# Second product of the last layer's Strassen down projection: P2 ahead of P3, and the P5 weight sums twelve units later

## The chip, the cores and the metric

One core of one Trainium2 chip runs the whole program. The metric is the device time of one execution in microseconds (us). The kernel before was run three times (median 2460.65 us), and one further execution was profiled.

## The reference

A bidirectional encoder trunk of two layers (`DEPTH = 2`) on 1040 rows (16 meta tokens and 1024 of the sequence), width 1024. Each layer is a hybrid mixer (a chunked gated delta rule beside a gated short convolution), then a SwiGLU feed-forward block with `D_FF = 2816` columns, that is 22 tiles of 128. Only the feed-forward block matters here:

```python
def swiglu(h, w_gate_up, w_down):
    gate, up = jnp.split(h @ w_gate_up.astype(h.dtype), 2, axis=-1)
    return (jax.nn.silu(gate) * up) @ w_down.astype(h.dtype)
...
    for l in range(DEPTH):
        h = h + hybrid_mixer(rmsnorm(h, norm1_w[l]), w_in[l], ...)
        h = h + swiglu(rmsnorm(h, norm2_w[l]), w_gate_up[l], w_down[l])
    h = rmsnorm(h, final_norm_w)
    return h[:, N_META:]
```

## The kernel before

**Arithmetic.** Every fp32 product is made of three fp32r matmuls: both operands are split into a rounded part (`hi`) and the remainder (`lo`), and `hi*hi + hi*lo + lo*hi` goes into one PSUM bank. The split of a tile is one ScalarE copy (`hi`) and one VectorE subtraction (`lo`). In the down projection these are lines L1320 and L1321 for weights (128x384, three tiles of 128) and L1368 and L1369 for activations (128x512); the three matmuls are L1688, L1690 and L1691.

**The down projection.** 18 of its 22 row tiles go through a two-level product scheme of Strassen's kind in Winograd's form: the 8 output tiles are two halves of four, the 18 inner tiles are two halves of nine (`NP = 9`), and the 1024 columns of the last layer are two halves of 512 (`NB = 512`, one PSUM bank, `NJ = 1`). Seven products `P1` to `P7` replace eight. The other four row tiles are multiplied plainly afterwards, together with the final norm.

**Units.** A product is 12 units: three blocks `b` of three inner tiles, and in each block four output tiles `m`. A unit is nine matmuls of 512 columns. `UNITS` lists all 84 in the order of `SEVEN`, which before is P5, P3, P2, P1, P6, P7, P4 in both layers. P5, P2 and P1 start new PSUM banks at `b == 0`, four for the four `m`. P3 goes on adding in the banks of P5 after P5 has been read out, and P6, P7 and P4 in those of P1. The read-outs are VectorE additions into the residual rows (L1695), four for each product, in the units of its last block. `pbank()` goes round the eight banks, so P5 and P1 get the same four and P2 gets the other four.

**Operands.** These are the preparations on VectorE that matter here, beside the splits:

- `s_sum("S2", n)`, L1279: loads a third weight block (192 KB, into a ring `s_room` of eight places) and subtracts it from the weight sum `S` which P5 has used. Twelve of them, one for each `n`. P3 and later P6 use the result.
- `w_unit` of a P3 unit, L1317: subtracts that sum `S` from a freshly loaded weight block. Twelve. The weights of P2 are plain loaded blocks (`a_raw`) without a subtraction; both come from the same ring of buffers.
- `t_pair` of a P3 tile, L1371: after the split, makes the second activation sum, which P6 uses, in place. Nine, one for each inner tile. P2 and P3 load their nine activation tiles through the same ring of seven places (`b_room`), from the rows that the gate/up part wrote to DRAM (`ad`).

**Order.** Work is written out unit by unit: `under[u]` lists what is issued ahead of the matmuls of unit `u`. Weights are split `LEAD = 5` units ahead of use. The twelve S2 sums stand under units 3 to 14; P3's first weights are made under unit 7. The helper `behind` puts such VectorE work of unit `u` after the read-out of unit `u - 2`, where there is one. A planner then lays out the queue of each engine from that order, as priorities, and its own estimates of durations, and the program holds the queues as laid out. Ahead of the first units stands the end of the gate/up part, whose last rows are finished by L1442 to L1445 and whose last banks are read out by L1573 to L1586.

```python
            if p in ("P5", "P6", "P7"):
                r = s_raw(n)
            elif p == "P3":
                r = a_raw(0, 1, n)
                behind(tt(out=r, in0=r, in1=s_raw(n), op=ALU.subtract))
            else:
                r = a_raw(*{"P2": (0, 1), "P1": (0, 0), "P4": (1, 1)}[p], n)
```

The part of the second layer runs from about 2209 us to 2398.8 us of the span. Its first units are interleaved with the last matmuls of gate/up until about 2230 us.

Of the kernel before, what the change touches and what calls it, by code (L numbers as in the profile page):

```python
# [42 lines left out]
def trunk(ctx: ExitStack, tc: tile.TileContext, xT, w_in, w_ba, w_out, w_gu, w_dn,  # L43
# [8 lines left out]
    def nm(p):  # L52
        cnt[0] += 1
        return f"{p}_{cnt[0]}"
# [13 lines left out]
    def bank(tag):  # L68
        return psp.tile([128, 512], F32, tag=tag, bufs={"acc": 3, "a": 1, "f": 2, "b": 2}[tag], name=nm("p" + tag))
# [15 lines left out]
    def after(ins, prev):  # L85

        if prev is not None:
            tc.add_manual_dep(ins.ins, prev.ins.name, dep, reason="order")
        return ins
# [51 lines left out]
    def wload(src, nk):  # L141

        res = []
        step = min(nk, WK)
        for k0 in range(0, nk, step):
            kk = min(step, nk - k0)
            hi = wp.tile([128, WK, 128], F32R, tag="whi", name=nm("whi"))
            lo = wp.tile([128, WK, 128], F32R, tag="wlo", name=nm("wlo"))
            wsplit(src[:, k0:k0 + kk, :], hi[:, 0:kk, :], lo[:, 0:kk, :])
            for k in range(kk):  # L150
                res.append((hi[:, k, :], lo[:, k, :]))
        return res
# [161 lines left out]
    for l in range(DEPTH):  # L314
        last = l == DEPTH - 1
# [722 lines left out]
        def half(ap, z):  # L1038

            v = ap.rearrange("p (g e) -> p g e", g=4) if len(ap.shape) == 2 else ap.rearrange("p k (g e) -> p k g e", g=4)  # L1040
            s = slice(1, 3) if z == 0 else slice(0, 4, 3)
            return v[:, s, :] if len(ap.shape) == 2 else v[:, :, s, :]
# [67 lines left out]
        def pbank():  # L1110
            bn[0] += 1
            return bank(("acc", "f", "acc", "b", "acc", "f", "b", "a")[bn[0] % 8])
# [21 lines left out]
        def part(t, z, j):  # L1134

            v = half(t[:, o0:L], z)
            return v[:, j, :] if NJ == 2 else v
# [6 lines left out]
        def pin(ps):  # L1144
            return loc(ps, 0)
# [86 lines left out]

        SEVEN = ("P5", "P3", "P2", "P1", "P6", "P7", "P4")
        BH = {"P2": (1, 0), "P3": (1, 1), "P1": (0, 0), "P7": (0, 0), "P4": (1, 0)}
        NBK = NP // 3
        UNITS = [(p, b, m) for p in SEVEN for b in range(NBK) for m in range(4)]
        td = dram.tile([NP, 128, NB], F32, name=nm("td"))
# [3 lines left out]
        def behind(ins):  # L1243

            return after(ins, read_out.get(at[0] - 2))
# [6 lines left out]
        def a_load(to, dh, fh, n):  # L1252
            f0 = NF + NP * fh + 3 * (n // 4)
            dma(to.rearrange("p (k e) -> p k e", k=3), w_dn[l, 4 * dh + n % 4, :, f0:f0 + 3, :])
            return to

        def a_raw(dh, fh, n):
            nr[0] += 1
            return a_load(raw4("raw" if nr[0] % 7 in (0, 3) else "ck2").rearrange("p a b -> p (a b)")[:, 0:384], dh, fh, n)

        def s_raw(n):
            r = n // 2
            if ("S", r) not in dw:
                dw["S", r] = row(Y[1], F32, 3) if r < 3 else c4k("S") if r < 5 else row(X[1] + "f")
            return dw["S", r][:, 384 * (n % 2):384 * (n % 2) + 384]

        def s_room():

            nr[2] += 1
            r = nr[2] // 2 % 4  # L1270
            if ("X", r) not in dw:
                dw["X", r] = row(X[1], F32, 3) if r < 3 else row(Y[1] + "f")
            return dw["X", r][:, 384 * (nr[2] % 2):384 * (nr[2] % 2) + 384]

        def s_sum(which, n):

            S = s_raw(n)
            if which == "S2":
                behind(tt(out=S, in0=S, in1=a_load(s_room(), 0, 0, n), op=ALU.subtract))  # L1279
            else:  # L1280
                behind(tt(out=S, in0=a_raw(1, 1, n), in1=S, op=ALU.subtract))
# [61 lines left out]
        def t_slot(t):  # L1343

            o = 2 * NB * (t % 4)
            return [dw["T", t // 4 % 2][:, o + NB * q:o + NB * q + NB] for q in range(2)]

        def t_load(t):
            p, i = SEVEN[t // NP], t % NP
            if p in BH:  # L1350
                dw["b", t] = b_load(*BH[p], i)
                held[t] = NB * ((nr[1] - 1) % 7)
            elif p == "P5":
                dma(t_raw(i), td[i])

        def t_pair(t):
            p, i = SEVEN[t // NP], t % NP
            hi, lo = t_slot(t)
            r = dw.pop(("b", t), None)
            held.pop(t, None)  # L1360
            if p in ("P5", "P6"):
                r = t_raw(i)
            elif p == "P7":
                behind(tt(out=r, in0=t_raw(i), in1=r, op=ALU.subtract))
            elif p == "P4":
                b21, r = r, t_raw(i)
                behind(tt(out=r, in0=b21, in1=r, op=ALU.subtract))
            act(out=hi, in_=r, func=AF.Copy)  # L1368
            behind(tt(out=lo, in0=r, in1=hi.bitcast(F32), op=ALU.subtract))  # L1369
            if p == "P3":  # L1370
                tt(out=t_raw(i), in0=r, in1=t_raw(i), op=ALU.subtract)  # L1371
# [2 lines left out]
        LEAD = 5  # L1374
        under = [[] for _ in UNITS]
        for n in range(12):
            under[n + 3].append(lambda n=n: s_sum("S2", n))
            under[n + 49].append(lambda n=n: s_sum("S3", n))
        for t in range(4, NP * 7):
            u = max(0, 4 * (t // 3 - 1) - 1 + t % 3)  # L1380
# [75 lines left out]
        for f in range(FT):  # L1456
# [45 lines left out]
            ps = {}  # L1502
# [142 lines left out]
        def last_weights(m):  # L1645
            if not fin_w:
                fin_w.append(flat(Y[0][2], F32R)[:, 0:4096].rearrange("p (m k e) -> p m k e", m=8, k=4))
                rows = [row(Y[1], F32R, 3) for _ in range(3)] + [row(Y[1] + "f", F32R)]
                fin_w.append([r[:, 512 * q:512 * q + 512].rearrange("p (k e) -> p k e", k=4) for r in rows for q in range(2)])
            hi, lo = fin_w[0][:, m], fin_w[1][m]  # L1650
            wsplit(w_dn[l, m, :, 0:NF, :], hi, lo, raw4(("raw", "ck2")[m % 2]))
            wds.append([(hi[:, k], lo[:, k]) for k in range(4)])
# [6 lines left out]
        bks, begun = {}, {}  # L1659
# [4 lines left out]
        for u, (p, b, m) in enumerate(UNITS):  # L1664
            if b == 1 and p in FIRST:
                dh, z = FIRST[p]
                q = 4 * dh + m
                after(dma(half(hr[q][:, o0:L], z), half(hd[q][:, o0:L], z)), begun[u - 2])
            at[0] = u
            for fn in under[u]:  # L1670
                fn()
            if last and u == 77:
                for q in range(KT):
                    last_weights(q)
            if not last and u >= len(UNITS) - 2:
                pre["dn", u - len(UNITS) + 2] = wload(w_dn[l, u - len(UNITS) + 2, :, 0:NF, :], NF)
            if p in ("P5", "P2", "P1") and b == 0:
                for j in range(NJ):
                    bks[m, j] = pbank()
            wh, wl = dw.pop(("w", u))  # L1680
            for j in range(NJ):
                ps = bks[m, j]
                cs = slice(CW * j, CW * j + CW)
                for k in range(3):
                    th, tl = t_slot(3 * (u // 4) + k)
                    st = p in ("P2", "P5", "P1") and b == 0 and k == 0
                    en = b == NBK - 1 and k == 2
                    one = mm(ps[:, :CW], wh[:, k, :], th[:, cs], start=st, stop=False, skip_group_check=True)  # L1688
                    begun.setdefault(u, one)
                    mm(ps[:, :CW], wh[:, k, :], tl[:, cs], start=False, stop=False, skip_group_check=True)  # L1690
                    mm(ps[:, :CW], wl[:, k, :], th[:, cs], start=False, stop=en, skip_group_check=True)  # L1691
                if b == NBK - 1:
                    dh, z, op = TO[p]
                    h = part(hr[4 * dh + m], z, j)
                    read_out[u] = tt(out=h, in0=pin(ps), in1=h, op=op)  # L1695
# [9 lines left out]
        else:  # L1705
# [22 lines left out]
            for (n0, n1) in FIN:  # L1728
                e = (n1 - n0) // 4
                sv = ss[:, n0:n1]  # L1730
                ps = bank("a")
# [100 lines left out]
```

## Time and profile before

| | |
|---|---|
| three runs | 2459.36, 2460.65, 2460.89 us |
| the profiled execution | 2459.55 us |
| its span, first to last instruction | 2457.7 us |
| TensorE busy (matmul) | 2435.8 us, 99% of the span |
| VectorE busy | 1827.4 us, 74% |
| ScalarE busy | 1079.5 us, 44% |
| mean DMA rate | 137 GB/s |

The 1.85 us between the span and the execution's time lie around the first and the last instruction. In the rows that follow, PE is TensorE, PEld its weight loads, DVE VectorE, ACT ScalarE, SP the queue that issues the DMAs. A timeline row gives start and duration in us, engine, line, operation, what is written from what, and in brackets the idle time of the engine before it and what ended that. A stretch row gives the stretch and its length, then for each engine the busy time and the instructions in it, the granted TensorE clock, the mean busy share of the DMA engines and GB/s. Durations of neighbouring instructions overlap; what one costs its engine is the distance from start to start.

### The profile page before, as it was taken

How to read it: one execution, taken by the hardware profiler on the slowest of the kernel's cores; microseconds unless marked ns; L12 is line 12 of the kernel's file. 1: busy time of each engine (PE TensorE's matmuls, PEld its weight loads, DVE VectorE, ACT ScalarE, POOL GpSimd, SP SyncE). 2: the span in 40 equal slices, each digit the busy share in tenths (PEclk: the TensorE clock that was granted, in tenths of full speed). 3: DMA queues.
4: the chain of work that ended last, by engine and by line, in shares of the span. 5: the costliest groups of instructions: out<-in, count | busy, mean ns of one | idle time of the engine just before them, and what ended most of it. 6: DMA issues, size and time to landing. Idle time of an engine off the chain costs nothing. (4 is left out here: it accounts for less than half of the span.)

```text
span 2457.7 us, 45163 instructions
## 1 busy us (share of the span) xinstructions
PE 2435.8 (99%) x17590; PEld 2254.1 (92%) x17590; DVE 1827.4 (74%) x3416; ACT 1079.5 (44%) x2020; POOL 65.8 (3%) x157
## 2 busy tenths in 40 slices
PE   9999999999999999999999999999999999999998
PEld 8999999999999999999999988999988888887887
DVE  6888345768888877877657984457798888878775
ACT  6654433536333333344445543345463333334544
POOL 0130000000000000000000200000000000000002
PEclk9999999999999999999999999999999999999999
DMA  4445344534323224675224453546343222347641
GB/s 134 155 154 178 122 140 151 165 111 147 102 91 105 93 77 137 216 237 154 89 83 148 160 170 107 157 133 205 112 142 108 91 95 99 123 136 245 198 134 69
DMA packets 201898, 336.32 MB, mean 137 GB/s; under 512 B 23468, under 2 KB 88420, under 8 KB 201684
## 3 DMA queue, kind: packets, MB, share of 16 engines
q1 hardware_dynamic: 173572, 294.88, 37.3%
q10 hardware_dynamic: 25936, 34.19, 4.4%
q0 software_dynamic: 2176, 4.36, 0.6%
q8 instruction: 138, 2.26, 0.4%
q14 instruction: 76, 0.62, 0.1%
HBM read 251.36 MB, written 81.99 MB: 136 GB/s over the span
## 5 line engine op out<-in xcount | busy, mean ns | idle before, releaser
L168 PE MATMUL pacc<-a,whi 128*128 128x346 f32 (+1 forms) x800 | 260.6, 327 | 0.9 <-ACT a L188 0.9
L170 PE MATMUL pacc<-a,wlo 128*128 128x346 f32 (+1 forms) x800 | 259.3, 325 | 0.0
L168 PE MATMUL pacc<-b,whi 128*128 128x346 f32 (+2 forms) x672 | 232.7, 347 | 0.0
L170 PE MATMUL pacc<-b,wlo 128*128 128x346 f32 (+2 forms) x672 | 231.6, 346 | 0.2 <-DVE wlo L139 0.2
L169 PE MATMUL pacc<-a,whi 128*128 128x346 f32 (+1 forms) x681 | 221.9, 326 | 0.2 <-DVE a L189 0.2
L138 ACT ACTIVATE whi<-raw 128x512 fp32r<-128x512 f32 x166 | 104.4, 631 | 238.4 <-PE pacc L169 193.5
L169 PE MATMUL pacc<-b,whi 128*128 128x346 f32 (+2 forms) x580 | 200.2, 346 | 0.0
L139 DVE TENSOR_TENSOR wlo<-raw,whi 128x512 fp32r<-128x512 f32 x166 | 114.0, 688 | 55.9 <-ACT whi L138 55.1
L168 PEld LDWEIGHTS pacc<-a,whi 128*128 128x128 f32 x800 | 150.8, 189 | 3.2 <-ACT a L188 1.2
L170 PEld LDWEIGHTS pacc<-a,wlo 128*128 128x128 f32 x800 | 150.9, 189 | 1.2 <-issue 0.8
L170 PEld LDWEIGHTS pacc<-b,wlo 128*128 128x128 f32 x672 | 126.5, 188 | 10.3 <-issue 1.7
L168 PEld LDWEIGHTS pacc<-b,whi 128*128 128x128 f32 x672 | 126.6, 188 | 10.1 <-issue 1.0
L169 PEld LDWEIGHTS pacc<-a,whi 128*128 128x128 f32 x681 | 128.5, 189 | 3.8 <-issue 2.1
L169 PEld LDWEIGHTS pacc<-b,whi 128*128 128x128 f32 x580 | 109.2, 188 | 7.8 <-issue 1.0
L1104 ACT ACTIVATE whi<-rw 128x512 fp32r<-128x512 f32 (+1 forms) x84 | 51.5, 621 | 104.1 <-PE pacc L1125 24.5
L1104 ACT ACTIVATE b<-rw 128x512 fp32r<-128x512 f32 (+1 forms) x63 | 38.8, 621 | 85.1 <-PE pb L1125 28.3
L1104 ACT ACTIVATE a<-rw 128x512 fp32r<-128x512 f32 (+1 forms) x63 | 38.8, 621 | 79.3 <-PE pacc L1125 22.5
L331 DVE TENSOR_TENSOR b<-pacc,rstd 128x346 f32<-128x346 f32 (+1 forms) x63 | 32.3, 512 | 48.5 <-PE pacc L170 45.9
L331 DVE TENSOR_TENSOR a<-pacc,rstd 128x346 f32<-128x346 f32 (+2 forms) x59 | 32.6, 553 | 41.5 <-PE pacc L170 41.4
L1105 DVE TENSOR_TENSOR wlo<-rw,whi 128x512 fp32r<-128x512 f32 (+1 forms) x84 | 56.1, 672 | 5.4 <-ACT whi L1104 5.1
L1688 PE MATMUL pacc<-P,whi 128*128 128x260 f32 (+1 forms) x177 | 59.6, 337 | 0.3 <-ACT whi L1320 0.3
L1691 PE MATMUL pacc<-P,wlo 128*128 128x260 f32 (+1 forms) x177 | 59.5, 336 | 0.0
(1143 smaller groups left out, 7948.6 us busy)
## 6 DMA issues: line engine op xcount, KB each, us to landing
raw<-in_w_in SPq DMA_DIRECT2D x110, 256.0 KB, 3.1
raw<-in_w_gu SPq DMA_DIRECT2D x108, 256.0 KB, 3.1
rw<-in_w_gu SPq DMA_DIRECT2D x88, 256.0 KB, 2.7
rw<-in_w_dn SPq DMA_DIRECT2D x90, 192.0 KB, 2.5
rec<-vkd SPq DMA_DIRECT2D x61, 256.0 KB, 4.3
raw<-in_w_out SPq DMA_DIRECT2D x48, 256.0 KB, 2.9
b<-ad SPq DMA_DIRECT2D x45, 260.0 KB, 4.4
a<-ad SPq DMA_DIRECT2D x45, 256.0 KB, 4.0
```

What stands on the lines that cost most here:

```text
L138: whi_done[0] = hasten(wpr, lambda: act(out=hi, in_=raw[:, 0:kk, :], func=AF.Copy))
L139: whi_done[1] = hasten(wpr, lambda: tt(out=lo, in0=raw[:, 0:kk, :], in1=hi.bitcast(F32), op=ALU.subtract))
L168: mm(ps[:, :n], wh, xh[:, n0:n1], start=(i == 0), stop=False)
L169: mm(ps[:, :n], wh, xl[:, n0:n1], start=False, stop=False)
L170: last_mm[0] = mm(ps[:, :n], wl, xh[:, n0:n1], start=False, stop=(i == K - 1))
L331: tt(out=t[:, n0:n1], in0=ps, in1=rstd[:, n0:n1], op=ALU.mult)
L1104: hasten(wpr, lambda: act(out=hi, in_=src, func=AF.Copy))
L1105: hasten(wpr, lambda: tt(out=lo, in0=src, in1=hi.bitcast(F32), op=ALU.subtract))
L1688: one = mm(ps[:, :CW], wh[:, k, :], th[:, cs], start=st, stop=False, skip_group_check=True)
L1691: mm(ps[:, :CW], wl[:, k, :], th[:, cs], start=False, stop=en, skip_group_check=True)
```

## The change

In the last layer alone, the order of the seven products becomes P5, P2, P3, P1, P6, P7, P4: the third comes second. The twelve S2 sums are listed under units 15 to 26 instead of 3 to 14. The banks of a product are looked up by whether it is P2, since P2 now runs while P5's banks wait for P3. The first layer keeps its order.

```diff
-        SEVEN = ("P5", "P3", "P2", "P1", "P6", "P7", "P4")
+        SEVEN = ("P5", "P2", "P3", "P1", "P6", "P7", "P4") if last else ("P5", "P3", "P2", "P1", "P6", "P7", "P4")
...
-            under[n + 3].append(lambda n=n: s_sum("S2", n))
+            under[n + (15 if last else 3)].append(lambda n=n: s_sum("S2", n))
...
-                    bks[m, j] = pbank()
+                    bks[p == "P2", m, j] = pbank()
...
-                ps = bks[m, j]
+                ps = bks[p == "P2", m, j]
```

## The prediction

> **What bounds the kernel now.** I read the page first, then the table of stretches over the last layer's down projection, cut at the starts of its products, and then the timelines of the stretch that stands out.
>
> ```profile
> span 2457.7 us, 45163 instructions
> PE 2435.8 (99%) x17590; PEld 2254.1 (92%) x17590; DVE 1827.4 (74%) x3416; ACT 1079.5 (44%) x2020; POOL 65.8 (3%) x157
> ```
>
> ```profile
> core 0: us, PE busy (x) PEld busy (x) DVE busy (x) ACT busy (x) POOL busy (x), PEclk, DMA share, GB/s
> 2209.00:2230.60 21.60, 21.60 (x95) 17.59 (x94) 18.76 (x30) 6.27 (x12) 0.00 (x0) 1.00 0.56 185
> 2230.60:2247.30 16.70, 16.70 (x74) 13.56 (x73) 15.02 (x28) 7.66 (x14) 0.00 (x0) 1.00 0.99 332
> 2247.30:2274.30 27.00, 25.85 (x110) 20.09 (x109) 24.40 (x46) 12.97 (x26) 0.00 (x0) 1.00 0.82 254
> 2274.30:2299.10 24.80, 24.80 (x109) 20.26 (x108) 15.33 (x26) 11.25 (x22) 0.00 (x0) 1.00 0.70 223
> 2299.10:2324.10 25.00, 25.00 (x110) 20.32 (x110) 19.97 (x34) 13.94 (x25) 0.00 (x0) 1.00 0.64 203
> ...
> 2374.00:2398.80 24.80, 24.80 (x109) 20.21 (x108) 15.71 (x27) 9.69 (x18) 1.33 (x5) 1.00 0.33 95
> ```
>
> TensorE bounds the program, so a change here is worth only what it takes off, or adds to, TensorE's idle time. The rows are: the seam with gate/up, the rest of P5, P3, P2, P1 and, after those left out, P4. P3's stretch is the only one with idle TensorE time (25.85 of 27.00 us), and there VectorE is busy 24.40 us; in P2's it is busy 15.33 of 24.80 us. The stretches of P1 and P4 have no idle TensorE time.
>
> Inside P3's stretch the timelines of TensorE, ScalarE and VectorE read:
>
> ```profile
> 2253.82 0.40 PE L1690 MATMUL pb<-P,a 128*128 128x512 f32 x1
> 2254.91 0.50 PE L1688 MATMUL pf<-P,a 128*128 128x512 f32 x1 [0.69 <-ACT a L1320]
> 2255.25 0.39 PE L1690 MATMUL pf<-P,a 128*128 128x512 f32 x1
> 2255.98 0.50 PE L1688 MATMUL pacc<-P,whi 128*128 128x512 f32 x1 [0.34 <-ACT whi L1320]
> 2256.32 0.40 PE L1690 MATMUL pacc<-P,whi 128*128 128x512 f32 x1
> 2256.83 0.51 PE L1691 MATMUL pb<-P,a 128*128 128x512 f32 x1
> 2257.18 0.40 PE L1688 MATMUL pb<-P,a 128*128 128x512 f32 x1
> ...
> 2258.35 0.40 PE L1691 MATMUL pb<-P,a 128*128 128x512 f32 x1
> ```
>
> ```profile
> 2254.33 0.52 ACT L1320 ACTIVATE a<-rw 128x384 fp32r<-128x384 f32 x1 [2.08 <-DVE rw L1317]
> 2255.40 0.94 ACT L1320 ACTIVATE whi<-rw 128x384 fp32r<-128x384 f32 x2 [0.55 <-DVE rw L1317]
> ```
>
> ```profile
> 2253.28 0.55 DVE L1321 TENSOR_TENSOR a<-rw,a 128x384 fp32r<-128x384 f32 x1
> 2253.75 0.55 DVE L1317 TENSOR_TENSOR rw<-rw,a 128x384 f32<-128x384 f32 x1
> 2254.22 0.68 DVE L1369 TENSOR_TENSOR P<-a,P 128x512 fp32r<-128x512 f32 x1
> 2254.82 0.55 DVE L1317 TENSOR_TENSOR rw<-rw,a 128x384 f32<-128x384 f32 x1
> ```
>
> TensorE waits for a split weight (L1320), the split waits for P3's weight subtraction (L1317), and that one stands in a VectorE queue without a gap: VectorE is late, by its amount of work. This is the one stall that the change can take away.
>
> **What the stall is worth.** From 2257.18 to 2258.35 five steps take 1.17 us, 0.234 us each. From 2253.82 to 2257.18 six steps take 3.36 us; at 0.234 they would take 1.40. The stall costs 1.96 us. This is more than the idle time shown (0.69 + 0.34), since the first matmul after each gap also takes longer and its successor starts later. Nothing else in this part can be gained: the other quoted stretches have no idle TensorE time. By the Trainium skill (TensorE: Matmul & The Clock Gate, "Wait — 56ns, not 53.3ns?") warm matmuls of 512 columns follow each other every 215.7 ns; with that figure the stall would be 2.07 us, an estimate, but the rows here say 0.234 us and they decide.
>
> **What moves away from the stall.** Stretches of VectorE for the three kinds of sums, one row pair each for L1279 (S2 sums), L1317 (P3's weights) and L1371 (the activation sums made with P3); the first row of a pair ends where the stall begins:
>
> ```profile
> 2209.00:2254.90 45.90, 5.34 (x10) 1.00 0.73 237
> 2254.90:2274.30 19.40, 1.10 (x2) 1.00 0.89 283
> 2209.00:2254.90 45.90, 3.92 (x8) 1.00 0.73 237
> 2254.90:2274.30 19.40, 2.68 (x5) 1.00 0.89 283
> 2209.00:2254.90 45.90, 6.17 (x9) 1.00 0.73 237
> 2254.90:2274.30 19.40, 0.00 (x0) 1.00 0.89 283
> ```
>
> An instruction of 384 columns occupies VectorE for 0.47 us (2253.28 to 2253.75) and one of 512 for 0.60 us (2254.22 to 2254.82). There are 12, 12 and 9 of them in all; one of L1317 crosses the cut and is in both its rows. By the stall VectorE had worked on 10 + 8 of the former and 9 of the latter: 18 x 0.47 + 9 x 0.60 = 13.9 us of work that P5 and P2 do not need. With P2 second, all of it belongs to a product that starts 24.8 us later. What P2 itself needs by then, one weight split a unit and three activation splits in four units, P3 needs as well, so it adds nothing. VectorE was late by about 2 us and is relieved of 13.9. I take the stall as gone, −1.96 us; the bounds are 0 (the relief is undone by something unseen) and −1.96.
>
> **What then falls due later.** P3's stage now has all 24 sums of 0.47 and nine of 0.60, 16.7 us, on top of what a plain product needs, 15.33 us (P2's row): 32.0 us of work in 24.8 us of TensorE time, 7.2 us too much. But P2's stage ahead of it leaves 24.80 − 15.33 = 9.5 us of VectorE free, and the two together need 47.4 of 49.6 us. The S2 sums can use that room: they stand under units 15 to 26, their ring has eight places, and each needs only its load and a sum that P5 has finished with. P3's weights are due five units ahead of use. The length of a unit follows from the starts of P2 and P1:
>
> ```profile
> 2274.27 0.39 PE L1688 MATMUL pb<-P,whi 128*128 128x512 f32 x1
> 2299.15 0.39 PE L1688 MATMUL pacc<-P,whi 128*128 128x512 f32 x1
> ```
>
> That is 24.88 us for 12 units, 2.07 us each, so the lead is 10.4 us, more than the 7.2 us even if no sum ran ahead. In the stage of before VectorE came from two stretches without slack (18.76 of 21.60 and 15.02 of 16.70 us) and still lost only 1.96 us. I cost this at 0, between 0 and +7.2 us; the cover is the lead, and if that were gone entirely the price would be the full 7.2.
>
> **Loads.** Each S2 sum brings a DMA of 192 KB, twelve in all, 2.36 MB, about 7.1 us at the 332 GB/s of the stretch from 2230.60, where the DMA engines are 0.99 busy. They leave that stretch for P2's stage, which at 0.70 of 24.8 us has 7.4 us free: just enough, and it need not all fit, since the ring lets loads go early. What waits for such a load is the sum itself, and behind it in VectorE's order the splits for P2 and P2's read-outs. On SP's queue the S2 loads pass P2's activation and weight loads, which now stand ahead of them. I cost this at 0 (a late load: up to the lead again).
>
> **Banks.** P2 now opens its banks twelve units earlier, at about 2247 us. They were gate/up's, and the last one is read out here:
>
> ```profile
> 2230.42 0.60 ACT L1582 ACTIVATE a3f<-pa 128x512 f32<-128x512 f32 x1
> ```
>
> That is 16 us earlier, so it costs nothing. P1 opens the banks that P3 has just left: before, P2's 12 units lay between, now there are three units (6.2 us) from the end of P3's unit for one `m` to P1's first matmul on the same bank. How late a read-out can be is seen at the worst one before, P5's last:
>
> ```profile
> 2247.08 0.40 PE L1691 MATMUL pf<-P,a 128*128 128x512 f32 x1
> ```
>
> ```profile
> 2251.61 0.68 DVE L1695 TENSOR_TENSOR b<-pf,b 128x512 f32<-128x512 f32 x1
> ```
>
> It ended 4.8 us after its last matmul, with VectorE full. This fits in 6.2 us, so the new wait costs 0; with VectorE as late as 7.2 us it would cost 1.0 us. In return P5's read-outs lose their haste, since P3 comes 12 units later. The reloads of residual rows ahead of each product's read-out change places with their product and cost nothing either way.
>
> **The sum.** −1.96 + 0 + 0 + 0 = −1.96 us. On the profiled execution that is 2459.55 − 1.96 = 2457.6 us, span 2455.7 us. That execution lies 1.1 us under the median of the three runs, so for a median I take 2460.65 − 1.96 = 2458.7 us. TensorE has no idle time between the stall and the end of the last quoted stretch, so nothing catches up with the gain before 2398.8 us; the plain end after it depends on TensorE's arrival in the same way. A measurement of this kernel can tell about 0.2% (4.9 us) from no change, and the gain is below that.
>
> **The rivals.** First, the stall moves instead of going: P3's stage, 12 units later, has the same weight sums and more, and the planner may leave them as late as before. For it speaks that 32.0 us of work still stand against 24.8; against it, the 9.5 us free just ahead. Its price is the old stall again, so the net is 0: 2460.65 us. I give it 0.18.
>
> Second, slower: VectorE enters P3's stage with nothing done ahead, because a sum waiting for its load holds the queue through P2's stage. Then 7.2 us of excess work meets a lead that is used up, and the result is 2460.65 − 1.96 + 7.2 = 2465.9 us. It is slower than now from the point where less than 7.2 − 1.96 = 5.2 us of the excess is covered away, and by more than 4.9 us only if nearly the whole lead is lost. For it speaks the tight sum of DMA time (7.1 of 7.4 us); against it, that the loads ran at 332 GB/s where they had to. With other disorder of a newly laid out queue I give it 0.11. By the Trainium skill (TensorE: Matmul & The Clock Gate, "HAM oscillation — how this bites in real kernels") TensorE gaps over about 3.4 us also lose the clock; a single gap of 7.2 us would then cost more than here. The stall above is shorter and its stretch keeps a clock of 1.00, so no row here tests that.
>
> Third, a gain above 4.9 us. The stretches of this part hold no more than the 1.96 us; it would have to come from the layout of the queues in the plain end, and no row speaks for it: 0.04. That the change does not do what it says (the planner runs the sums early anyway, in holes) leaves the forecast standing, since P2 does not wait for them.
>
> **How the numbers follow.** The forecast has 0.67: 2458.7 us, with its own range from 2457.2 to 2460.9, the spread of the runs and a stall only partly gone. With the first rival it makes 0.85 within 0.2%; slower 0.11, faster 0.04. For 8 in 10 the range takes in the first rival and part of the way to the second: 2456.8 to 2463.0.
>
> **What would show it.** In the profile after, the TensorE timeline from 2247 us on should have steps of 0.234 us without a gap, P2's matmuls following P5's, and no L1317 before about 2255 us. In P2's stage VectorE should be fuller than 15.33 us by S2 sums, and P3's stage, from about 2272 us, should have idle TensorE time of 0 with L1317 ahead of its splits. P1's first matmuls should not wait for L1695. The forecast is wrong if a TensorE gap released by L1320 or L1321 stands in P3's stage, by the length of that gap, or if one stands where the rows of before show none.

## The result: 0.14% faster, TensorE's stall gone, and more saved than the stall of one profile

In 22 runs of each kernel in turn, the median went from 2459.02 us (2456.30 to 2461.77) to 2454.82 us (2453.10 to 2462.09), 4.2 us less. The ratio is 0.9986, with a 95% interval from 0.9980 to 0.9991: between 2.2 and 4.9 us faster. The change thus stays within the 0.2% that the prediction called no change, but the time lies 2.0 us under its range (2456.8 to 2463.0).

The first profiled execution of the changed kernel was the slowest of all its runs (2462.09 us; half clock for 3.41 us at 56 and at 210 us, where the queues of both kernels are still the same). A second profile of it, of 2454.03 us, is read here. Its stretches from 2226.90 us are the rest of P5, then P2, P3 and P1, which answer to the table of before:

```profile
core 0: us, PE busy (x) PEld busy (x) DVE busy (x) ACT busy (x) POOL busy (x), PEclk, DMA share, GB/s
2226.90:2243.90 17.00, 17.00 (x75) 13.83 (x74) 12.79 (x23) 8.62 (x17) 0.00 (x0) 1.00 0.85 281
2243.90:2268.80 24.90, 24.90 (x109) 20.27 (x108) 22.93 (x43) 10.02 (x20) 0.00 (x0) 1.00 0.75 233
2268.80:2293.70 24.90, 24.90 (x109) 20.27 (x108) 18.71 (x35) 12.12 (x24) 0.00 (x0) 1.00 0.74 232
2293.70:2318.30 24.60, 24.60 (x108) 20.01 (x107) 19.68 (x34) 13.19 (x25) 0.00 (x0) 1.00 0.64 201
```

TensorE has no idle time in any of them; before, P3's stretch had 25.85 us busy of 27.00. VectorE's work is levelled: P3's stage holds 18.71 us instead of 24.40, P2's 22.93 instead of 15.33, and the DMA engines are 0.85 busy in the stretch of P5 where they were at 0.99. The seam from P3 to P1 on the timelines of TensorE and VectorE, in the same profile:

```profile
2293.49 0.40 PE L1691 MATMUL pf<-P,a 128*128 128x512 f32 x1
2293.73 0.39 PE L1688 MATMUL pacc<-P,whi 128*128 128x512 f32 x1
```

```profile
2289.99 0.68 DVE L1695 TENSOR_TENSOR b<-pacc,b 128x512 f32<-128x512 f32 x1
...
2294.84 0.68 DVE L1695 TENSOR_TENSOR b<-pf,b 128x512 f32<-128x512 f32 x1
```

P1 starts 0.24 us after P3's last matmul, on a bank that was read out 3 us earlier. P3's last read-out ends 1.6 us after its matmul, where P5's had taken 4.8 us before.

From its first to its last matmul (L1688 to L1691) the part takes 187.58 us in all three profiles of the changed kernel. In the profile of before that the prediction used it took 189.61 us: 2.03 us saved, by the sum's 1.96. The measured median moved twice as far, 4.2 us. The experiments below look for the rest.

### The profile page after: what moved, and what is told of

Same layout as the page of the kernel before. It is cut to its first block, busy times and chain, and to the rows that moved or that the text cites. A ratio compares the mean times of both kernels' runs of the same rounds, so it can differ in the third digit from the quotient of the medians.

```text
span 2460.3 us, 45153 instructions
## 1 busy us (share of the span) xinstructions
PE 2438.8 (99%) x17590; PEld 2257.0 (92%) x17590; DVE 1826.4 (74%) x3416; ACT 1078.8 (44%) x2020; POOL 66.3 (3%) x157
## 5 line engine op out<-in xcount | busy, mean ns | idle before, releaser
L331 DVE TENSOR_TENSOR a<-pacc,rstd 128x346 f32<-128x346 f32 (+2 forms) x59 | 32.6, 553 | 41.7 <-PE pacc L170 41.6
L1691 PE MATMUL pacc<-P,wlo 128*128 128x260 f32 (+1 forms) x177 | 59.5, 336 | 0.0
L1688 PE MATMUL pacc<-P,whi 128*128 128x260 f32 (+1 forms) x177 | 59.4, 336 | 0.0
```

What stands on the lines that cost most here:

```text
L331: tt(out=t[:, n0:n1], in0=ps, in1=rstd[:, n0:n1], op=ALU.mult)
```

## The experiments

Each one is compared with the kernel before in the same session. "Part" is the time from the first to the last matmul of the scheme in the second layer, read from the one profile of each.

| kernel | part, us | ratio to before | 95% interval |
|---|---|---|---|
| before, again | 189.92 | 0.9996 | 0.9988 to 1.0005 |
| changed, again | 187.58 | 0.9981 | 0.9973 to 0.9990 |
| changed, third time | 187.58 | 0.9990 | 0.9981 to 0.9998 |
| order only | 187.55 | 0.9984 | 0.9975 to 0.9992 |
| before without S2 loads | 187.78 | 0.9988 | 0.9980 to 0.9996 |
| before without second activation sums | 187.56 | 0.9988 | 0.9979 to 0.9996 |
| before with 24 more VectorE instructions | 200.77 | 1.0039 | 1.0026 to 1.0051 |
| changed with the same 24 | 191.40 | 1.0005 | 0.9996 to 1.0014 |

**Both kernels again.** No edit.

> The kernel before, unchanged, once more, for the spread of its stall at the head of P3. Work theory (VectorE is late by its amount of work, and by how much differs between executions): ratio 1.000, and a TensorE stall in P3's stretch that differs clearly from the 1.96 us of the first profile, 3 to 5 us where the execution is slower. Rival (the stall is always 2 us and the rest of the 0.14% comes from elsewhere): ratio 1.000 and again 2 us of stall.

> The changed kernel, unchanged, once more, for a profile with the clock granted as in the kernel before. Work theory: ratio 0.998 to 0.999, no TensorE gap from the start of P5's own stretch to the end of P4, the part about 187.6 us long from its first to its last matmul as in the first profile. Rival: the part is as long, and a further 1.5 to 2 us are saved after it, in the plain end, or before it.

Before again had the same stall, 2.3 us (part 189.92). The changed kernel again had none. After the part, from its last matmul to the end of the span, the two profiles take 59.20 and 59.10 us, so nothing is saved in the plain end. This left the further difference unexplained by either theory as put.

**The order without the later sums.**

```diff
-            under[n + (15 if last else 3)].append(lambda n=n: s_sum("S2", n))
+            under[n + 3].append(lambda n=n: s_sum("S2", n))
```

> P2 second as in the change, but the twelve S2 sums listed under units 3 to 14 as before. Work theory: 8 weight subtractions and 9 activation sums still leave the stage before P2, 3.8 + 5.4 = 9.2 us of VectorE time, against a lateness of 2 to 5 us: the stall is gone and the ratio is that of the change, 0.9980 to 0.9991. Load theory (the twelve loads of 192 KB in the stretch with the DMA engines 0.99 busy make the weights late): part of the stall stays, ratio 0.999 to 1.000.

The stall is gone, as with the whole change, at a ratio that cannot be told from it. The order alone does it. The listing of the sums matters little, because the planner does not hold to it: in the changed kernel eight of the twelve sums (L1279) start between 2226.34 and 2243.48 us, ahead of P2's stage, which is as many as their ring has places; two more start at the end of P2's stage and two in P3's.

**The kernel before without the loads of the S2 sums.**

```diff
-                behind(tt(out=S, in0=S, in1=a_load(s_room(), 0, 0, n), op=ALU.subtract))
+                behind(tt(out=S, in0=S, in1=s_raw(n - 1 if n else 1) if last else a_load(s_room(), 0, 0, n), op=ALU.subtract))
```

> The kernel before, but each S2 sum of the last layer takes a weight sum that lies in SBUF already in place of its loaded block (the twelve loads of 192 KB are left out; VectorE's work is the same). Work theory: the stall stays, ratio 0.9995 to 1.0005. Load theory: the stall goes or is halved, ratio 0.998 to 0.9992.

The stall is 0.2 us, against the work theory: VectorE's work is the same and the stall has gone nevertheless. VectorE's timeline shows what became of the sums:

```profile
2211.13 0.55 DVE L1279 TENSOR_TENSOR a<-a 128x384 f32<-128x384 f32 x1
...
2212.67 0.55 DVE L1279 TENSOR_TENSOR a<-a 128x384 f32<-128x384 f32 x1
2213.14 0.55 DVE L1317 TENSOR_TENSOR rw<-rw,a 128x384 f32<-128x384 f32 x1
2213.61 0.55 DVE L1279 TENSOR_TENSOR a<-a,a 128x384 f32<-128x384 f32 x1
2214.07 0.55 DVE L1317 TENSOR_TENSOR rw<-rw,a 128x384 f32<-128x384 f32 x1
```

They stand in the seam with gate/up, from 2211 us on, and P3's weight subtractions follow them at once. In the kernel before, the same timeline reads:

```profile
2215.87 0.69 DVE L1371 TENSOR_TENSOR a<-a,a 128x512 f32<-128x512 f32 x1 [2.75 <-DMA a<-ad]
...
2234.53 0.55 DVE L1279 TENSOR_TENSOR a<-a,b 128x384 f32<-128x384 f32 x1
...
2236.60 0.55 DVE L1317 TENSOR_TENSOR rw<-rw,a 128x384 f32<-128x384 f32 x1
...
2239.30 0.69 DVE L1371 TENSOR_TENSOR a<-a,a 128x512 f32<-128x512 f32 x1 [1.68 <-DMA a<-ad]
```

The first S2 sum starts at 2234.53 us and the first weight subtraction at 2236.60. VectorE stood idle for 2.75 us ahead of 2215.87 and for 1.68 us ahead of 2239.30. At the first of these there was no sum to fill it with, since the loads for the sums were issued only from 2229.95 us on. So the loads have a part in the stall, by when they come. It was not DMA time that held the first of them back. Shortly ahead of their issue the DMA engines were 0.20 busy:

```profile
2224.20:2227.70 3.50, 3.50 (x17) 2.83 (x16) 3.50 (x6) 0.51 (x1) 0.00 (x0) 1.00 0.20 56
```

In that stretch SP's queue waited 3.5 us for VectorE to finish a row of gate/up (L1445) that it had to store (L1449). Whether the buffers of the loads were free any sooner, and whether DMA time made the later loads late, was not told apart.

**The kernel before without the second activation sums.**

```diff
-            if p == "P3":
+            if p == "P3" and not last:
                 tt(out=t_raw(i), in0=r, in1=t_raw(i), op=ALU.subtract)
```

> The kernel before, with the nine second activation sums of the last layer's P3 left out (P6 then uses the first ones): 5.4 us less VectorE work ahead of the stall, all loads kept. Work theory (VectorE's lateness of about 2 us makes the stall): the stall is gone, the part is 187.6 us long, ratio 0.9985 to 0.9992. Load theory (the weights are late through the twelve loads of the S2 sums): the stall stays near 2 us, ratio 0.9995 to 1.0005.

With every load kept and 5.4 us of VectorE work gone, the stall is gone as well; the stretch of P3:

```profile
2246.00:2270.90 24.90, 24.90 (x110) 20.25 (x109) 20.62 (x39) 12.29 (x26) 0.00 (x0) 1.00 0.78 251
```

The two experiments together say that the stall is a shortage of VectorE time by some 2 us, which either less work or sums that can be done earlier make good.

**More VectorE work, with no more loads.** The same edit in both kernels:

```diff
-                behind(tt(out=r, in0=r, in1=s_raw(n), op=ALU.subtract))
+                for op in (ALU.subtract, ALU.add, ALU.subtract) if last else (ALU.subtract,):
+                    behind(tt(out=r, in0=r, in1=s_raw(n), op=op))
```

> The kernel before with each of P3's twelve weight subtractions of the last layer made three times (minus, plus, minus): 24 more VectorE instructions of 0.47 us, 11.3 us, no more loads. Work theory: seven to eight of the twelve come before the stall, so 7 to 11 us of added work meet a VectorE that is already late, and the stall grows from 2 to between 8 and 13 us: ratio 1.002 to 1.0045. Load theory: the stall grows by less than 3 us, ratio below 1.0015.

> The changed kernel with the same 24 added VectorE instructions, 11.3 us, which fall in the P2 and P3 stages. By the sum of the prediction the two stages then hold 47.4 + 11.3 = 58.7 us of VectorE work in 49.6 us, 9.1 us over, against a lead of 10.4 us: no stall or up to 2 us, ratio to the kernel before 0.998 to 0.9993. If the lead is mostly used up already (the prediction's slower rival), the stall is 5 to 9 us and the ratio 1.000 to 1.002.

In the kernel before, 11.3 us of added work lengthen the part by 11.2 us (189.61 to 200.77). VectorE was late already, but that the two numbers agree is chance in part: 2.9 us of the 11.2 are half clock behind the last wait, as shown below, and 8.3 us are what the part grew by up to that wait. In the changed kernel the added work lengthens it by 3.8 us (187.58 to 191.40), with no half clock, so the new order absorbs 7.5 us. That was more stall than the sum gave (up to 2 us) and less than the slower rival's (5 to 9). The timed runs agree: about 9.6 us (0.39%) more than before for the one, and for the other 3.6 us more than the changed kernel's third set of runs in the same session (2459.19 against 2455.63 us).

The first of the two held a surprise. Its TensorE timeline and the stretches of its stall (lines stand one higher in this kernel from L1317 on):

```profile
2248.95 0.40 PE L1691 MATMUL pb<-P,a 128*128 128x512 f32 x1
2251.68 0.50 PE L1689 MATMUL pacc<-P,whi 128*128 128x512 f32 x1 [2.33 <-ACT whi L1321]
...
2254.33 0.79 PE L1692 MATMUL pb<-P,a 128*128 128x512 f32 x1 [1.83 <-DVE a L1322]
2254.92 0.63 PE L1689 MATMUL pb<-P,a 128*128 128x512 f32 x1
2255.35 0.63 PE L1691 MATMUL pb<-P,a 128*128 128x512 f32 x1
...
2263.12 0.79 PE L1689 MATMUL pf<-P,a 128*128 128x512 f32 x1 [3.14 <-ACT a L1321]
...
2269.26 0.39 PE L1692 MATMUL pf<-P,a 128*128 128x512 f32 x1
```

```profile
2245.00:2252.18 7.18, 4.85 (x21) 3.49 (x19) 7.18 (x14) 2.92 (x5) 0.00 (x0) 1.00 0.45 137
2252.18:2259.01 6.83, 5.00 (x13) 3.59 (x12) 6.83 (x15) 0.00 (x0) 0.00 (x0) 0.50 0.68 209
2259.01:2262.43 3.42, 0.97 (x4) 0.45 (x3) 3.42 (x8) 0.52 (x1) 0.00 (x0) 1.00 0.30 84
2262.43:2269.25 6.82, 6.13 (x14) 4.79 (x15) 6.31 (x14) 3.64 (x8) 0.00 (x0) 0.50 0.56 158
```

It has three waits, of 2.33, 1.83 and 3.14 us. From 2252.18 us, just behind the first, and from 2262.43 us, within the third, the granted clock is halved for 6.8 us each, and matmuls follow each other every 0.43 us instead of 0.23. Behind the last wait fourteen steps take 6.14 us (2263.12 to 2269.26), where the full clock would take 3.25: 2.9 us more. A stall here can cost more than its own length.

**The clock.** Over all timed runs the mean granted clock was 0.9979 and 0.9980 for the kernel before (35 and 27 runs) and 0.9984 for the changed one in each of its three sets. 0.0005 of 2456 us is 1.2 us, most of the 1.4 us by which the first ratio (3.4 us) exceeds the 2.03 us of the part.

> The changed kernel unchanged, a third time, for the granted clock. In the runs so far its mean granted clock was 0.9984, that of the kernel before 0.9979, worth 1.5 us, and at an equal clock the two differ by 2.0 to 2.5 us. If the difference in clock is chance, the clock of this one comes out within 0.0002 of the kernel before in the same session and the ratio near 0.9991; if it belongs to the change, the clock differs by 0.0005 again and the ratio is 0.998 to 0.9986.

The clock differed by 0.0004 again, while the ratio came out at 0.9990, as for chance. The question was then whether the short stall of the kernel before can halve the clock as well. Four more profiles were taken of it, unchanged:

> The kernel before, unchanged, for one more profile of its stall. Clock theory (where the stall falls in one of the clock's steps of 3.41 us it is long enough, in some executions, to halve the clock for the next step or two, 1.7 us each, as the stalls of 2.5 and 3.3 us did in the kernel with 24 added instructions): in one or two of the four looks a stretch of half clock stands within 5 us behind the stall, and the part is 191.3 us or longer. Chance theory (the lower mean clock of the kernel before comes from half-clock steps in code that both kernels share): no half clock there in any of the four, the part 189.5 to 190 us long.

> As the look before it: half clock behind the stall in some of the four looks (clock theory), or in none (chance theory).

> As the looks before it: half clock behind the stall in some of the four looks (clock theory), or in none (chance theory).

> As the looks before it: half clock behind the stall in some of the four looks (clock theory), or in none (chance theory).

The parts took 190.05, 191.13, 191.43 and 189.75 us. One of the four, the third, has the half clock behind its stall; timeline of TensorE and stretches:

```profile
2249.10 0.40 PE L1690 MATMUL pb<-P,a 128*128 128x512 f32 x1
2250.47 0.50 PE L1688 MATMUL pf<-P,a 128*128 128x512 f32 x1 [0.97 <-ACT a L1320]
2250.81 0.39 PE L1690 MATMUL pf<-P,a 128*128 128x512 f32 x1
2251.54 0.50 PE L1688 MATMUL pacc<-P,whi 128*128 128x512 f32 x1 [0.34 <-ACT whi L1320]
2251.88 0.40 PE L1690 MATMUL pacc<-P,whi 128*128 128x512 f32 x1
2252.39 0.50 PE L1691 MATMUL pb<-P,a 128*128 128x512 f32 x1
2252.73 0.48 PE L1688 MATMUL pb<-P,a 128*128 128x512 f32 x1
2253.01 0.63 PE L1690 MATMUL pb<-P,a 128*128 128x512 f32 x1
2253.44 0.63 PE L1691 MATMUL pb<-P,a 128*128 128x512 f32 x1
```

```profile
2249.47:2252.88 3.41, 1.99 (x7) 1.04 (x7) 3.41 (x8) 1.99 (x4) 0.00 (x0) 1.00 0.80 222
2252.89:2256.30 3.41, 3.41 (x9) 2.63 (x9) 3.41 (x8) 0.53 (x1) 0.00 (x0) 0.50 1.00 320
2256.30:2259.70 3.40, 3.40 (x16) 2.77 (x16) 2.47 (x5) 2.73 (x5) 0.00 (x0) 1.00 0.93 331
```

There are nine matmuls in the 3.41 us of half clock instead of 15 or so: the same stall, then 1.7 us more. The second of the four had no half clock there, but a longer stall. One of its waits is

```profile
2250.29 0.40 PE L1690 MATMUL pb<-P,a 128*128 128x512 f32 x1
2252.56 0.50 PE L1688 MATMUL pf<-P,a 128*128 128x512 f32 x1 [1.87 <-ACT a L1320]
```

where the first profile had 0.69 us idle for the same matmul. So the stall differs between executions of one program. The six profiles of the kernel before give parts of 189.61 to 191.43 us, 190.3 us in the mean, and the change takes 2.7 us off that mean, a ratio of 0.9989. This lies in all three intervals of the changed kernel.

What stays open is the last 0.7 us to the 3.4 us of the first ratio, which the intervals do not need. No run shows that it comes from the clock: the kernel with the order only has no stall either and a mean clock of 0.9980, and half-clock steps stand far from the stall in profiles of both kernels (at 205 us in the first of the four, at 56 and 210 us in the first profile of the changed kernel).

## Why the prediction was wrong in its time and right in its mechanism

**What bounds, and the stall.** This was right. TensorE's only idle time in this part was in P3's stretch, by VectorE's lateness, and it is gone with P2 second.

**What the stall is worth: the step that failed.** The term of −1.96 us was taken from one execution and treated as a constant, with 0 and −1.96 as its bounds. In six executions the part ran 2.0 to 3.9 us longer than in the changed kernel, 2.7 in the mean, so the term that the profiles support is −2.7 us. The medians lie 4.2 us apart and the ratio says 3.4; what these have beyond 2.7 is found in no stretch. The profiled execution on record was the one with the smallest excess. The prediction asked of its terms what happens when a cover fails, and never what the stall itself might be in another run. The statement that no row tested the loss of the clock was true, but it was used only to make a slower case dearer. The same loss belonged to the kernel before, as part of the possible gain.

**The base.** The sum set out from 2460.65 us, the median of three runs, and treated their spread of 1.5 us as the spread of the kernel. The 22 runs have a median of 2459.02 and a spread of 5.5 us. So 1.6 us of the distance from 2458.7 to 2454.82 is base, and 2.2 us is the size of the gain (4.2 us between the medians against 1.96).

**What falls due later.** No stall came, as forecast, but by another account. P2's and P3's stages hold 22.93 + 18.71 = 41.6 us of VectorE work, not 47.4, mainly since eight S2 sums (3.8 us) ran ahead of both. P2's stage was indeed fuller than 15.33 us, but not by S2 sums, as the prediction had it: seven of P3's weight subtractions (L1317, 3.69 us) and eight activation sums (L1371, 5.51 us) stand there. And the lead was overrated. By the prediction's sum, 47.4 + 11.3 = 58.7 us in 49.6 us of TensorE time, the 9.1 us over should have gone into the 10.4 us of lead. By the rows above, 41.6 + 11.3 = 52.9 us in 49.8 us are 3.1 us over, an estimate, and the part still grew by 3.8. On this estimate the cover was VectorE's free time in the two stages, and nothing of the lead can be seen. The slower rival may thus have been nearer than its 0.11 suggested, though the change as it stands does not reach it.

**Loads.** The prediction put the S2 loads at 0 and named them only as a risk in their new place. Without them the kernel before loses its stall, so when they come was part of what made it. Nor did they leave P5's stretch, since eight of the twelve sums ran ahead of P2's stage. VectorE's queue without a gap at 2253 us showed only that VectorE was late then, not why it had not begun sooner. Its idle 2.75 us ahead of 2215.87 us were the row to ask about.

**Banks.** This was right: TensorE does not wait for L1695 ahead of P1, and P3's last read-out comes sooner after its matmul than P5's had before.

**The first rival, the stall moved on,** did not come about; nor did the second. The listing of the S2 sums, half of the change, turned out to be worth nothing measurable beside the order.

**The chances.** The ratio of 0.9986 lies within 0.2%, where 0.85 was put. That it did is no credit to the size of the term.

## What to carry to other kernels

A stall read from one profile is a sample. Before costing its removal, profile the unchanged program a few times, and let the range for the gain reach to the longest stall seen and to a step of lost clock behind it. Where an engine is late, look for its idle time ahead of the lateness and ask what it was missing there; here a better order, less work or earlier operands each cured the same 2 us. To learn how much cover a new order really has, add work to the engine in both versions: 11.3 us cost 11.2 in the one (2.9 of it half clock) and 3.8 in the other.

## What the hardware showed that was not expected

TensorE's clock can halve for a step of 3.41 us after less idling than a whole step. In the third of the four further profiles no single wait exceeded 0.97 us, and the step ahead of the half clock had 1.99 us busy of 3.41 with seven matmuls. How much of a step is idle does not decide it alone. In the second of the four, whose steps are counted back here in multiples of 3.41 us from a change of its clock at 2450.17 us, one step was idle for longer and the next kept the full clock (in the third, the changes at 2252.89 and 2447.45 us lie on one such count):

```profile
2248.78:2252.20 3.42, 1.83 (x7) 0.85 (x5) 3.42 (x8) 0.74 (x2) 0.00 (x0) 1.00 0.61 173
2252.20:2255.61 3.41, 2.59 (x9) 1.52 (x10) 3.41 (x8) 1.77 (x4) 0.00 (x0) 1.00 0.86 260
```

What does decide it stays open. The Trainium skill (TensorE: Matmul & The Clock Gate, "HAM oscillation — how this bites in real kernels") states as the rule that there be no TensorE-idle gaps over about 3.4 us; the third profile differs, with 0.97 us as the longest gap. In the kernel before with 24 more VectorE instructions the clock changed at 2252.18, 2259.01, 2262.43 and 2269.25 us, one or two times 3.41 us apart, as the Trainium skill has it (TensorE: Matmul & The Clock Gate, "What's actually happening").
